# A two-block transformer on one core: background steps held back from a feed-forward layer's first granules, and the second mixer's norm outputs, bias rows and constants placed elsewhere

## The chip, the core and the metric

The kernel runs on one core of a Trainium2 chip. The core has a matmul engine (TensorE, PE in the profile; its weight loads are PEld), three elementwise engines (VectorE is DVE, ScalarE is ACT, GpSimd is POOL), a sync engine (SP) that issues most of the loads, and 16 DMA engines. Each engine takes its instructions strictly in the order of its own queue, so an instruction that waits holds up all that stand behind it. The metric is the device time of one execution in microseconds (us); lower is better.

## The reference

One sequence of 256 tokens of width 1024 passes two blocks, all in float32. The first block has two layers, each of four steps with a layer norm behind the first, second and last:

```python
x = layer_norm(ALPHA*x + 0.5*swiglu(x, ffn1_up, ffn1_down))   # width 2816
x = layer_norm(ALPHA*x + token_mix(x))                        # four branches, gates, w_out
x = x + ple_gate(x) * (p @ w_ple)
x = layer_norm(ALPHA*x + 0.5*swiglu(x, ffn2_up, ffn2_down))
```

The second block begins with a modulation that depends on one vector c alone:

```python
mod = silu(c) @ w_ada + b_ada                  # 6 x 1024: shift, scale, gate; twice
h = rms_norm(x, norm_mix) * (1 + sc_m) + sh_m
x = x + g_m * hybrid_mixer(h, ...)             # differential attention, LRU, sliding window
h = rms_norm(x, norm_ffn) * (1 + sc_f) + sh_f
x = x + g_f * moe_ffn(h, ...)                  # 32 experts
```

The hybrid mixer needs a table of relative-position biases (`rel_bias`, by distance), a scalar and a gain for the differential attention, and products of query and key gains.

## The kernel before, in words

The 256 tokens are two tiles t of 128. A float32 product is made of three matmuls: each weight and each activation is split into a high part (`hi`, on ACT, L161, tile `whi`) and the rest (`lo`, L165, tile `wlo`), and PE adds xh*hi, xh*lo and xl*hi (L223 to L225). Weights come in **granules** of 128 x 1024: SP loads one into `raw` (4 buffers), ACT and DVE split it into `whi` and `wlo` (7 buffers, and 4 more in an extra pool while a feed-forward layer runs). `onpool` names the granules of a product whose `lo` half is split on POOL instead of DVE.

A feed-forward layer (`ffn`) goes through its 2816 columns in six blocks; each block has a product with the first half of the up weights and one with the second half, 8 granules in all. On DVE the first is gated (L325) and multiplied with the second (L329), and PE transposes the result (L251, tile `th`). The first block makes both products for t=0 and then for t=1 (`gemms`); its granules on POOL are `pl1` for the first half and `pl2` for the second. Then come 22 granules of down weights; the last eight are used for all of t=0 and then for all of t=1, and the layer norm of a tile follows its last product: residual (L284), statistics (L285, L287), a reciprocal root of small steps (L142 to L156), scaling (L292, L293), transposes (L251).

The modulation is computed beside the first block: `ada` is a generator that multiplies 32 pieces of `w_ada` (tile `araw`, two buffers) by c and adds them up in `acc`, one piece a step (L842), eight steps to an `acc`. It runs as three background jobs (`self.bg`): in the first layer's first feed-forward (`ada(0, 4)`), its second (`ada(4, 8)`) and the second layer's first (`ada(8, 12)`). After each granule that it loads, `load_split` calls `self.background(1)`, which runs the job to its next `yield`.

This sets the order in which the program is written. A scheduler then orders each engine's queue by what is ready in its own reckoning; an instruction that is not tied by data can move ahead of what is written before it. `pin` keeps an instruction in the order in which it was written.

At the end of the first block `load_first` loads the first product of the mixer and `norm_first` computes its norm (L879, L884, L885) into two of the four `raw` buffers. `hybrid` then makes the bias rows (`rel_rows`: two small matmuls, L995, and DMAs through DRAM), the products dq and dk for t=0 and t=1, dv, the differential attention (`diff_attn`, with its constants; the key norm ends with L1067), then r, the LRU and the window attention. The mixture of experts follows; it streams its weights in tiles of 1 MB (`mraw`) into memory that the earlier stages free.

Of the kernel before, what the change touches and what calls it, by code (L numbers as in the profile page):

```python
# [71 lines left out]
class Kernel:  # L72
    def __init__(self, tc, a, out, dbg=None):
        self.tc, self.nc, self.a, self.out, self.dbg = tc, tc.nc, a, out, dbg
        self.n = 0
        self.nraw, self.nhl, self.next, self.xp = 4, 7, 4, None
        self.npj, self.ngt, self.glag = 4, 4, 1
        self.dtail = 8
        self.xg = 4
        self.sp, self.late = None, False  # L80
        self.pre, self.npre = [], 5
        self.start = False
        self.na, self.nb = 8, 9
# [726 lines left out]
    def ada(self, r0, r1):  # L810
# [3 lines left out]
        with self.tc.tile_pool(name=self.nm("ada"), bufs=1, side="right") as pool:  # L814
# [169 lines left out]
    def rel_rows(self, mp):  # L984

        nc, a = self.nc, self.a
        rel = self.st(mp, [33, 12], "rel")
        nc.vector.memset(rel[32:33, :], -1e30)
        nc.gpsimd.dma_start(rel[0:32, :], a["rel_bias_2"])
        oh = self.st(mp, [33, 2, 384], "s4")  # L990
        nc.gpsimd.dma_start(oh, a["bucket"])
        row = self.st(mp, [12, 2, 384], "s4")
        for i in range(2):
            pr = self.ps("sc")
            nc.tensor.matmul(pr[:12, :384], rel, oh[:, i, :], start=True, stop=True)  # L995
# [33 lines left out]
    def gain128(self, a1, a2):  # L1029
# [6 lines left out]
        gp = self.small(1, "g1")  # L1036
        self.pin(nc.vector.tensor_tensor(gp, g[:, 0:1], g[:, 1:2], op=OP.mult))
        return gp

    def diff_attn(self, mp, dq, dk, dv):  # L1040
        nc, a = self.nc, self.a
        lv = self.st(mp, [P, 4, 64], "s2")
        src = a["diff_lambda_2"][0]
        nc.gpsimd.dma_start(lv, bass.AP(tensor=src.tensor, offset=src.offset, ap=[[0, P], [64, 4], [1, 64]]))
        lp = self.st(mp, [P, 2, 64], "s2")
        nc.vector.tensor_tensor(lp, lv[:, 0::2, :], lv[:, 1::2, :], op=OP.mult)
        ls = self.small(2, "lz")
        nc.vector.tensor_reduce(ls, lp, axis=AX.X, op=OP.add)
        nc.scalar.activation(ls, ls, AF.Exp)
        nlam = self.small(1, "nl")  # L1050
        nc.vector.tensor_tensor(nlam, ls[:, 1:2], ls[:, 0:1], op=OP.subtract)
        nc.vector.tensor_scalar(nlam, nlam, -LAMBDA_INIT, None, op0=OP.add)
        gsub = self.st(mp, [P, P], "s2")
        nc.gpsimd.dma_start(gsub, arow(a["diff_subln_2"][0], P))
        nc.vector.tensor_scalar(gsub, gsub, 1.0 - LAMBDA_INIT, None, op0=OP.mult)
        gp = self.gain128(a["diff_qnorm_2"][0], a["diff_knorm_2"][0])
# [71 lines left out]
    def swa(self, mp, sq_, kv):  # L1128
# [3 lines left out]
        gp = self.gain128(a["swa_qnorm_2"][0], a["swa_knorm_2"][0])  # L1132
# [61 lines left out]
    def hybrid(self, ctx, first):  # L1194
# [3 lines left out]
        with tc.tile_pool(name="mix2", bufs=1, reuse_waits="tile") as mp:  # L1198
            self.mod_cols()

            self.st(mp, [33, 12], "rel")
# [8 lines left out]
            with tc.tile_pool(name="scr", bufs=1, reuse_waits="tile") as self.sp:  # L1210
                self.rel_rows(mp)
                dq, dk = self.projs(mp, lhs, w, (1024, 512, (), first), (1536, 512, (2, 3), None))
# [5 lines left out]
                for i in range(2):  # L1218
                    r = self.proj(mp, lhs, w, i * 512, 512, onpool=(1, 3))
# [613 lines left out]
    def run(self):  # L1833
        nc, a, tc = self.nc, self.a, self.tc
        with tc.tile_pool(name="const", bufs=1) as self.cp, tc.tile_pool(name="small", bufs=2) as self.smp, \
# [15 lines left out]
            def load_first():  # L1851
                first.extend(self.load_split(KD, a["w_in_2"][0], 1024, 512, onpool=(1,2,3)))

            def norm_first(t):
                if self.dbg != "ln3_1":
                    hs.append(self.st(self.wp, [P, D], "raw", bufs=self.nraw))
                    self.rms_mod(t, hs[t], A, sh)

            with tc.tile_pool(name="ln", bufs=1) as self.lnp:
                pl, self.pl1, self.pl2 = (self.pl1, self.pl2), (), ()  # L1860
                for L in range(2):
# [3 lines left out]
                    if L:  # L1865
                        self.bg = self.ada(8, 12)
# [11 lines left out]
                    if L == 0:  # L1878
                        self.bg = self.ada(4, 8)
# [56 lines left out]
```

## Time and profile before

| what | value |
|---|---|
| time, median of 3 runs (lowest to highest) | 2527.62 us (2524.69 to 2527.79) |
| the profiled execution: its own time, its span | 2525.59 us, 2524.0 us |
| granted TensorE clock, mean | 0.98 |
| busy: PE, DVE, ACT, POOL | 95%, 52%, 33%, 8% |
| moved by DMA | 705.94 MB, mean 280 GB/s |

The span begins with the first instruction of the execution and ends with the last; times within it are counted from its start. The layer norms that matter here end at about 217 and 225 us (layer 0, first feed-forward), 666 and 684 us (layer 0, second) and 1306 and 1320 us (layer 1, second); the mixture of experts runs from about 1556 us to the end.

### The profile page before, as it was taken

The numbers are of one execution on the slowest core, as the hardware profiler recorded it, in microseconds if no ns is written. First come the engines' busy times: TensorE is split into PE (matmuls) and PEld (weight loads), VectorE is DVE, ScalarE is ACT, GpSimd is POOL, SyncE is SP. The second block draws the span as 40 slices with busy tenths as digits, with TensorE's granted clock in tenths as the row PEclk, the third lists the DMA queues.
The fourth block names the chain that finished last, engine by engine and source line by source line (L and its number), as shares of the span: only waits on it lengthen the run. The fifth ranks groups of instructions, "written<-read, shape, count | busy, mean of one in ns | idle before, by whom it ended". The sixth has DMA issues, their size and how long they took to land.

```text
span 2524.0 us, 29376 instructions
## 1 busy us (share of the span) xinstructions
PE 2389.5 (95%) x11078; PEld 1562.4 (62%) x11078; DVE 1313.9 (52%) x2243; ACT 827.1 (33%) x1227; POOL 209.1 (8%) x191
## 2 busy tenths in 40 slices
PE   8998999999799999999988999999999999999998
PEld 6887787778678878878877877433333333333332
DVE  7768757666666676675566775322222222222222
ACT  5443544444345454444435753100000001000000
POOL 4000211200200011230013010000000000000000
PEclk9999999999899999999998999999999999999999
DMA  8777465567666656566547467999999999999997
GB/s 272 242 236 233 144 188 182 184 215 222 210 188 215 217 159 175 171 197 195 184 131 232 118 199 289 399 421 421 420 421 421 420 421 420 420 421 421 421 421 325
DMA packets 202027, 705.94 MB, mean 280 GB/s; under 512 B 18122, under 2 KB 31642, under 8 KB 152984
## 3 DMA queue, kind: packets, MB, share of 16 engines
q1 hardware_dynamic: 194584, 684.02, 74.1%
q0 software_dynamic: 7296, 19.99, 2.7%
q8 instruction: 89, 1.46, 0.2%
q14 instruction: 58, 0.48, 0.1%
HBM read 702.83 MB, written 3.47 MB: 280 GB/s over the span
## 4 chain that ended last, share of the span: by engine, by line
PE 53%; DMA 31%; DVE 9%; issue 3%; ACT 3%; POOL 1%; SPq 0%; ACTq 0%; DVEq 0%; POOLq 0%
DMA mraw<-in_w_dram 25%; PE mm L225 12%; PE mm L224 12%; PE mm L223 12%; PE mm L1590 5%; PE sc L1621 4%; PE tp L251 3%; DVE wlo L165 2%; DMA araw<-in_w_ada_dram 2%; DMA raw<-in_ffn_up_dram 2%; ACT whi L161 1%; DMA raw<-in_w_in_dram 1%; PE tp L1700 1%; PE sc L1519 1%; DVE x L292 1%
## 5 line engine op out<-in xcount | busy, mean ns | idle before, releaser
L165 DVE TENSOR_TENSOR wlo<-raw,whi 128x1024 fp32r<-128x1024 f32 (+1 forms) x451 | 559.0, 1246 | 277.2 <-ACT whi L161 274.5
L161 ACT ACTIVATE whi<-raw 128x1024 fp32r<-128x1024 f32 x478 | 500.7, 1055 | 521.5 <-PE mm L225 386.3
L224 PE MATMUL mm<-wlo,xTh 128*128 128x512 f32 (+2 forms) x1520 | 580.4, 382 | 10.6 <-POOL wlo L165 8.6
L223 PE MATMUL mm<-whi,xTh 128*128 128x512 f32 (+2 forms) x1520 | 585.8, 386 | 2.1 <-ACT whi L161 1.7
L225 PE MATMUL mm<-whi,xTl 128*128 128x512 f32 (+2 forms) x1520 | 579.8, 382 | 0.0
L1590 PE MATMUL mm<-mraw,xe 128*64 128x512 f32 x1920 | 488.5, 613 | 33.6 <-DMA mraw<-in_w_dram 33.5
L1590 PEld LDWEIGHTS mm<-mraw,xe 128*64 128x64 f32 x1920 | 150.6, 141 | 332.6 <-issue 265.2
L224 PEld LDWEIGHTS mm<-wlo,xTh 128*128 128x128 f32 x1520 | 288.6, 190 | 69.8 <-POOL wlo L165 11.5
L223 PEld LDWEIGHTS mm<-whi,xTh 128*128 128x128 f32 x1520 | 289.0, 190 | 56.2 <-ACT whi L161 3.0
L225 PEld LDWEIGHTS mm<-whi,xTl 128*128 128x128 f32 x1520 | 288.6, 190 | 50.0
L1601 ACT ACTIVATE mt<-mg 128x256 f32<-128x256 f32 x64 | 26.6, 416 | 691.5 <-DVE mg L1600 689.5
L1621 PE MATMUL sc<-mraw,xTl 128*64 128x512 f32 x976 | 231.5, 597 | 7.4 <-ACT xe L1530 7.4
L1600 DVE TENSOR_SCALAR mg<-mm 128x256 f32<-128x256 f32 x64 | 27.2, 424 | 323.4 <-PE mm L1590 319.0
L1621 PEld LDWEIGHTS sc<-mraw,xTl 128*64 128x64 f32 x976 | 69.1, 137 | 125.6 <-issue 108.9
L225 PE MATMUL mm<-whi,hl 128*128 128x512 f32 x352 | 138.1, 392 | 0.0
L223 PE MATMUL mm<-whi,hh 128*128 128x512 f32 x352 | 137.6, 391 | 0.0
L224 PE MATMUL mm<-wlo,hh 128*128 128x512 f32 x352 | 137.5, 391 | 0.0
L1626 DVE TENSOR_TENSOR xTh<-sc,gf 128x512 f32<-128x512 f32 x32 | 22.1, 692 | 208.4 <-PE sc L1621 208.4
L1701 DVE TENSOR_TENSOR x<-x,tp 128x512 f32<-128x512 f32 x68 | 46.8, 688 | 129.8 <-PE tp L1700 129.8
L842 DVE SCALAR_TENSOR_TENSOR acc<-araw,cond,acc 128x512 f32<-128x512 f32 x96 | 72.8, 758 | 54.2 <-DMA araw<-in_w_ada_dram 51.8
L165 POOL TENSOR_TENSOR wlo<-raw,whi 128x1024 fp32r<-128x1024 f32 x27 | 68.9, 2564 | 285.6 <-ACT whi L161 285.5
L225 PEld LDWEIGHTS mm<-whi,hl 128*128 128x128 f32 x352 | 66.4, 189 | 13.6
(445 smaller groups left out, 2277.5 us busy)
## 6 DMA issues: line engine op xcount, KB each, us to landing
mraw<-in_w_dram SPq DMA_DIRECT2D x360, 1024.0 KB, 19.8
raw<-in_ffn_up_dram SPq DMA_DIRECT2D x176, 512.0 KB, 4.4
raw<-in_w_in_dram SPq DMA_DIRECT2D x142, 512.0 KB, 4.4
raw<-in_ffn_down_dram SPq DMA_DIRECT2D x88, 512.0 KB, 4.0
araw<-in_w_ada_dram SPq DMA_DIRECT2D x96, 256.0 KB, 3.6
AS<-in_w_dram SPq DMA_DIRECT2D x22, 1024.0 KB
raw<-in_w_branch_dram SPq DMA_DIRECT2D x28, 512.0 KB, 3.9
raw<-in_w_out_dram SPq DMA_DIRECT2D x16, 512.0 KB, 3.7
```

What stands on the lines that cost most here:

```text
L161: ins = self.nc.scalar.activation(hi, src, AF.Copy)
L165: ins = (self.nc.gpsimd if pool else self.nc.vector).tensor_tensor(lo, src, hi, op=OP.subtract)
L223: nc.tensor.matmul(banks[b], xh, hi[:, s], start=kc == 0, stop=False)
L224: nc.tensor.matmul(banks[b], xh, lo[:, s], start=False, stop=False)
L225: nc.tensor.matmul(banks[b], xl, hi[:, s], start=False, stop=kc == nk - 1)
L251: self.nc.tensor.transpose(pt[:s.shape[-1], i * P:i * P + s.shape[0]], s, self.ident)
L842: nc.vector.scalar_tensor_tensor(acc, raw, self.cond[:, k:k + 1], acc, op0=OP.mult, op1=OP.add)
L1590: self.pe(nc.tensor.matmul(ph[nb][e * 64:e * 64 + 64], xe[:, k, e * 64:e * 64 + 64], units[e][k][:, nb * 512:nb * 512 + 512], start=False, ...
L1600: nc.vector.tensor_scalar(g, pv[:, :, 0], 7.0, None, op0=OP.min)
L1601: nc.scalar.activation(th, g, AF.Tanh, scale=0.851)
L1621: self.pe(self.nc.tensor.matmul(py[c][e * 64:e * 64 + 64], aT[:, k:k + 64], units[e][j][:, o:o + 512], start=j == 0 and r == 0, stop=j == ...
L1701: nc.vector.tensor_tensor(self.x[t][:, s], self.x[t][:, s], po, op=OP.add)
```

## The change

Eight edits, in the order of the file. `pl1` loses both granules on POOL and `pl2` two of four. `self.hold` lets the first 12 calls of `background(1)` pass without a step, for `ada(4, 8)` and `ada(8, 12)`. `ada` yields once before its first step and once a step (before: twice behind every second one), and its first step is pinned. After the last job come the bias rows and the constants of the differential attention, with `araw` and `acc` as their working tiles and lasting tiles (`self.cp`) for their results; some of their arithmetic goes to POOL. The products of gains are made there too. `load_first` has granule 3 on DVE, dk has no granule on POOL, the first r product has none. `norm_first` writes into `whi` buffers of the extra pool.

```diff
-        self.pl1, self.pl2 = (2, 3), (0, 1, 2, 3)
-        self.bg = iter(())
+        self.pl1, self.pl2 = (), (1, 3)
+        self.bg, self.hold = iter(()), 0
...
     def background(self, n):
+        if n == 1 and self.hold:
+            self.hold -= 1
+            return
         for _ in range(n):
...
             nxt, last, ahead = start(r0), None, load(r0 * KD)
+            yield
...
-                    nc.vector.scalar_tensor_tensor(acc, raw, self.cond[:, k:k + 1], acc, op0=OP.mult, op1=OP.add)
+                    ins = nc.vector.scalar_tensor_tensor(acc, raw, self.cond[:, k:k + 1], acc, op0=OP.mult, op1=OP.add)
+                    if (i, k) == (r0, 0):
+                        self.pin(ins)
...
                     yield
-                    if j % 2:
-                        yield
                 last = i, acc
             yield
             finish(*last)
+            if r1 == 12:
+                yield
+                yield from self.rel_rows(lambda: self.st(pool, [P, 512], "araw", bufs=2),
+                                         lambda: self.st(pool, [P, 512], "acc", bufs=2))
...
-    def rel_rows(self, mp):
+    def rel_rows(self, one, two):
...
         for i in range(2):
-            pr = self.ps("sc")
-            nc.tensor.matmul(pr[:12, :384], rel, oh[:, i, :], start=True, stop=True)
-            nc.scalar.activation(row[:, i, :], pr[:12, :384], AF.Copy)
-        dr = self.dram.tile([12, 768], F32, name="relrow")
-        nc.gpsimd.dma_start(dr, row.rearrange("p a b -> p (a b)"))
+            oh = one()[:33, :384]
+            nc.gpsimd.dma_start(oh, a["bucket"][:, i])
+            row = two()[:12, :384]
+            pr = self.ps("tp")
+            nc.tensor.matmul(pr[:12, :384], rel, oh, start=True, stop=True)
+            nc.scalar.activation(row, pr[:12, :384], AF.Copy)
+            nc.gpsimd.dma_start(dr[:, i * 384:i * 384 + 384], row)
+            yield
...
+        nc.gpsimd.tensor_tensor(lp, lv[:, 0::2, :], lv[:, 1::2, :], op=OP.mult)
+        yield
+        ls = self.small(2, "lz")
+        self.pin(nc.vector.tensor_reduce(ls, lp, axis=AX.X, op=OP.add))
...
-                dq, dk = self.projs(mp, lhs, w, (1024, 512, (), first), (1536, 512, (2, 3), None))
+                dq, dk = self.projs(mp, lhs, w, (1024, 512, (), first), (1536, 512, (), None))
...
-                    r = self.proj(mp, lhs, w, i * 512, 512, onpool=(1, 3))
+                    r = self.proj(mp, lhs, w, i * 512, 512, onpool=(1, 3) if i else ())
...
-                first.extend(self.load_split(KD, a["w_in_2"][0], 1024, 512, onpool=(1,2,3)))
+                first.extend(self.load_split(KD, a["w_in_2"][0], 1024, 512, onpool=(1, 2)))
...
-                    hs.append(self.st(self.wp, [P, D], "raw", bufs=self.nraw))
+                    hs.append(self.st(self.xp, [P, D], "whi", F32R, bufs=self.next).bitcast(F32))
...
-                        self.bg = self.ada(8, 12)
+                        self.bg, self.hold = self.ada(8, 12), 12
...
-                        self.bg = self.ada(4, 8)
+                        self.bg, self.hold = self.ada(4, 8), 12
```

The diff alone does not show what becomes of the queues, so three places of DVE's queue follow. **Place 1**, before: the layer norm of t=0 at the end of layer 0's second feed-forward (`x_71` is the activation of t=0, `mm` a product, `acc` and `araw` the background job's tiles).

```order
L284 SCALAR_TENSOR_TENSOR x_71<-mm_5353,x_71 128x512
L285 BN_STATS bn_1201_5573<-x_71 128x6
L842 SCALAR_TENSOR_TENSOR acc_5925<-araw_6014,cond,acc_5925 128x512
L842 SCALAR_TENSOR_TENSOR acc_5925<-araw_6029,cond,acc_5925 128x512
L284 SCALAR_TENSOR_TENSOR x_71<-mm_5354,x_71 128x512
L842 SCALAR_TENSOR_TENSOR acc_5925<-araw_6038,cond,acc_5925 128x512
```

The same place in the changed kernel:

```order
L284 SCALAR_TENSOR_TENSOR x_71<-mm_5353,x_71 128x512
L285 BN_STATS bn_1201_5573<-x_71 128x6
L284 SCALAR_TENSOR_TENSOR x_71<-mm_5354,x_71 128x512
L285 BN_STATS bn_1201_5573<-x_71 128x6
L287 BN_AGGR mv_1202_5578<-bn_1201_5573 128x2
```

No background step stands in this norm any more; the same holds at the end of layer 0's first feed-forward. **Place 2**, before: the third block of layer 0's second feed-forward, from the gating of one product (L325) to the multiplication (L329) that its transposes wait for. `wlo` is the split of a granule on DVE.

```order
L325 SCALAR_TENSOR_TENSOR th_4541<-th_4541,mm_4491 128x512
L842 SCALAR_TENSOR_TENSOR acc_4556<-araw_4580,cond,acc_4556 128x512
L325 SCALAR_TENSOR_TENSOR th_4544<-th_4544,mm_4492 128x512
L842 SCALAR_TENSOR_TENSOR acc_4556<-araw_4659,cond,acc_4556 128x512
L165 TENSOR_TENSOR wlo_4671<-raw_4668,whi_4670 128x1024
L165 TENSOR_TENSOR wlo_4680<-raw_4677,whi_4679 128x1024
L842 SCALAR_TENSOR_TENSOR acc_4556<-araw_4674,cond,acc_4556 128x512
L842 SCALAR_TENSOR_TENSOR acc_4556<-araw_4683,cond,acc_4556 128x512
L165 TENSOR_TENSOR wlo_4745<-raw_4742,whi_4744 128x1024
L842 SCALAR_TENSOR_TENSOR acc_4556<-araw_4754,cond,acc_4556 128x512
L329 TENSOR_TENSOR th_4541<-th_4541,mm_4583 128x512
```

In the changed kernel the fourth block reads as follows, and the fifth likewise (L328 and L332 are the old L325 and L329, L846 is the old L842):

```order
L328 SCALAR_TENSOR_TENSOR th_4724<-th_4724,mm_4674 128x512
L846 SCALAR_TENSOR_TENSOR acc_4662<-araw_4736,cond,acc_4662 128x512
L328 SCALAR_TENSOR_TENSOR th_4727<-th_4727,mm_4675 128x512
L846 SCALAR_TENSOR_TENSOR acc_4662<-araw_4745,cond,acc_4662 128x512
L165 TENSOR_TENSOR wlo_4856<-raw_4853,whi_4855 128x1024
L846 SCALAR_TENSOR_TENSOR acc_4662<-araw_4754,cond,acc_4662 128x512
L165 TENSOR_TENSOR wlo_4865<-raw_4862,whi_4864 128x1024
L846 SCALAR_TENSOR_TENSOR acc_4662<-araw_4763,cond,acc_4662 128x512
L165 TENSOR_TENSOR wlo_4877<-raw_4874,whi_4876 128x1024
L846 SCALAR_TENSOR_TENSOR acc_4662<-araw_4842,cond,acc_4662 128x512
L165 TENSOR_TENSOR wlo_4942<-raw_4939,whi_4941 128x1024
L332 TENSOR_TENSOR th_4724<-th_4724,mm_4766 128x512
```

Before, half of each of the two later jobs stands ahead of its layer, in the norm before it and the work around that, and the other 16 steps are spread over the third to the fifth block; now all 32 steps stand between the first block and the first down granules. The second block has ten steps in a row between the L332 of the first block and its own, five of them behind its L328. **Place 3**, before: the end of the first block, where the norm of t=0 for the mixer (L884, L885) stands ahead of the residual of t=1 (`x_72`).

```order
L156 SCALAR_TENSOR_TENSOR ry_2378_10985<-rt_2380_10989,ry_2378_10985 128x1
L884 SCALAR_TENSOR_TENSOR raw_10974<-x_71,ry_2378_10985,AS_9538 128x512 x2
L885 TENSOR_TENSOR raw_10974<-raw_10974,AS_9538 128x512 x2
L284 SCALAR_TENSOR_TENSOR x_72<-mm_10728,x_72 128x512
L285 BN_STATS bn_2385_11064<-x_72 128x6
```

In the changed kernel the residual and statistics of t=1 stand among the root of that norm (L887 is the old L879), and three granules of dk stand in the layer norm of t=0 ahead of them:

```order
L165 TENSOR_TENSOR wlo_11234<-raw_11231,whi_11233 128x1024
L156 SCALAR_TENSOR_TENSOR ry_2380_11006<-rt_2382_11010,ry_2380_11006 128x1
L152 SCALAR_TENSOR_TENSOR rt_2382_11010<-ry_2380_11006,rh_2381_11008 128x1
L156 SCALAR_TENSOR_TENSOR ry_2380_11006<-rt_2382_11010,ry_2380_11006 128x1
L293 SCALAR_TENSOR_TENSOR x_71<-x_71,ry_2380_11006,lnb_10616 128x512 x2
L284 SCALAR_TENSOR_TENSOR x_72<-mm_10777,x_72 128x512
L887 TENSOR_TENSOR sr_2386_11024<-sr_2386_11024 128x1
L284 SCALAR_TENSOR_TENSOR x_72<-mm_10778,x_72 128x512
L142 TENSOR_SCALAR rv_2389_11030<-sr_2386_11024 128x1
L285 BN_STATS bn_2398_11113<-x_72 128x6
```

What was one norm behind the other is now the two in turns, with L892 and L893 (the old L884 and L885) of t=0 behind both L292 of t=1.

## Rows read from the trace of the kernel before

**Rows 1.** Windows: length, busy PE, PEld, DVE, ACT, POOL, granted clock, DMA share, GB/s.

```profile
190.00:240.00 50.00, 42.79 (x193) 36.32 (x192) 38.53 (x79) 18.90 (x29) 2.69 (x5) 0.90 0.68 218
640.00:700.00 60.00, 45.54 (x193) 37.28 (x192) 41.76 (x62) 20.97 (x25) 15.84 (x8) 0.89 0.60 189
850.00:890.00 40.00, 39.74 (x190) 33.68 (x189) 26.42 (x52) 16.82 (x24) 2.71 (x5) 1.00 0.52 165
1296.00:1384.00 88.00, 72.64 (x316) 58.05 (x314) 62.81 (x125) 38.19 (x68) 26.21 (x22) 0.90 0.53 171
1556.00:2524.00 968.00, 911.09 (x4080) 350.78 (x4078) 259.70 (x632) 87.44 (x227) 0.52 (x1) 0.97 1.00 413
```

**Rows 2.** Waits of PE, 190 to 240 us: us in total, times, longest.

```profile
PE tp L251 <- DVE x L293: 7.2, 1, 7.2
```

**Rows 3.** Waits of PE, 640 to 700 us.

```profile
PE tp L251 <- DVE x L293: 14.5, 2, 8.1
```

**Rows 4.** Timeline of DVE, 634 to 712 us: start, us, [idle before].

```profile
653.79 2.60 DVE L842 SCALAR_TENSOR_TENSOR acc<-araw,cond,acc 128x512 f32<-128x512 f32 x2 [7.09 <-DMA araw<-in_w_ada_dram]
...
660.57 0.74 DVE L292 SCALAR_TENSOR_TENSOR x<-x,mv,lng 128x512 f32<-128x512 f32 x1
...
673.92 2.32 DVE L292 SCALAR_TENSOR_TENSOR x<-x,mv,lng 128x512 f32<-128x512 f32 x1
```

**Rows 5.** Timeline of POOL, 640 to 700 us.

```profile
670.92 7.56 POOL L165 TENSOR_TENSOR wlo<-raw,whi 128x1024 fp32r<-128x1024 f32 x3 [15.87 <-ACT whi L161]
```

**Rows 6.** Waits of PE, whole span.

```profile
PE mm L224 <- POOL wlo L165: 8.6, 7, 1.6
...
PE tp L251 <- DVE raw L885: 6.1, 2, 3.4
...
PE tp L251 <- DVE s L1067: 5.5, 1, 5.5
...
PE sc L995 <- ACT sc L878: 1.5, 1, 1.5
```

**Rows 7.** Timeline of PE, 1296 to 1330 us.

```profile
1310.69 1.94 PE L251 MATMUL tp<-ident,raw 128*128 128x128 f32 x8 [2.74 <-DVE raw L885]
...
1325.37 1.94 PE L251 MATMUL tp<-ident,raw 128*128 128x128 f32 x8 [3.38 <-DVE raw L885]
```

**Rows 8.** Window of DVE, 1297.3 to 1325.4 us: length, busy.

```profile
1297.30:1325.40 28.10, 25.35 (x75) 0.92 0.19 50
```

**Rows 9.** Timeline of DVE, 1350 to 1364 us.

```profile
1355.66 2.38 DVE L154 TENSOR_TENSOR rt<-ry 128x32 f32<-128x32 f32 x1
...
1358.53 0.19 DVE L154 TENSOR_TENSOR rt<-ry 128x32 f32<-128x32 f32 x1
```

**Rows 10.** Waits of PE, 440 to 640 us.

```profile
PE mm L224 <- POOL wlo L165: 3.9, 3, 1.6
PE tp L251 <- DVE th L329: 3.0, 1, 3.0
```

**Rows 11.** Waits of PE, 700 to 860 us.

```profile
PE tp L251 <- DVE th L329: 1.3, 1, 1.3
```

**Rows 12.** Groups by form: xcount | busy, mean ns of one | idle before.

```profile
L842 DVE SCALAR_TENSOR_TENSOR acc<-araw,cond,acc 128x512 f32<-128x512 f32 x96 | 72.8, 758 | 54.2 <-DMA araw<-in_w_ada_dram 51.8 <-DMA acc<-in_b_ada_dram 1.8 <-DVE wlo L165 0.2
...
L165 DVE TENSOR_TENSOR wlo<-raw,whi 128x1024 fp32r<-128x1024 f32 x443 | 551.0, 1251 | 272.6 <-ACT whi L161 270.0
...
L165 POOL TENSOR_TENSOR wlo<-raw,whi 128x1024 fp32r<-128x1024 f32 x27 | 68.9, 2564 | 285.6 <-ACT whi L161 285.5
```

**Rows 13.** Timeline of DVE, 490 to 560 us: background steps.

```profile
526.87 0.75 DVE L842 SCALAR_TENSOR_TENSOR acc<-araw,cond,acc 128x512 f32<-128x512 f32 x1
...
546.98 0.75 DVE L842 SCALAR_TENSOR_TENSOR acc<-araw,cond,acc 128x512 f32<-128x512 f32 x1
```

**Rows 14.** Timeline of PE, 459.8 to 480 us.

```profile
459.83 0.39 PE L225 MATMUL mm<-whi,xTl 128*128 128x512 f32 x1
...
471.61 0.39 PE L223 MATMUL mm<-whi,xTh 128*128 128x512 f32 x1
```

More of the change, by code (lines that the diff above doesn't have):

```diff
@@ L982, in lru @@
             self.split_from(h[:, :, t * P:t * P + P], yT[t][0], yT[t][1])
-    def rel_rows(self, mp):
+    def rel_rows(self, one, two):
         nc, a = self.nc, self.a
-        rel = self.st(mp, [33, 12], "rel")
-        nc.vector.memset(rel[32:33, :], -1e30)
+        rel = self.cp.tile([33, 12], F32, name="rel")
+        nc.gpsimd.memset(rel[32:33, :], -1e30)
         nc.gpsimd.dma_start(rel[0:32, :], a["rel_bias_2"])
-        oh = self.st(mp, [33, 2, 384], "s4")
-        nc.gpsimd.dma_start(oh, a["bucket"])
-        row = self.st(mp, [12, 2, 384], "s4")
+        dr = self.dram.tile([12, 768], F32, name="relrow")
         for i in range(2):
-            pr = self.ps("sc")
-            nc.tensor.matmul(pr[:12, :384], rel, oh[:, i, :], start=True, stop=True)
-            nc.scalar.activation(row[:, i, :], pr[:12, :384], AF.Copy)
-        dr = self.dram.tile([12, 768], F32, name="relrow")
-        nc.gpsimd.dma_start(dr, row.rearrange("p a b -> p (a b)"))
+            oh = one()[:33, :384]
[6 more added lines that the diff above has]
+            yield
         self.skew = []
@@ L1005, in rel_rows @@
             self.skew.append(sk)
+        yield
+        lv, lp = one(), two()
+        lv, lp = lv[:, :256].rearrange("p (i d) -> p i d", i=4), lp[:, :128].rearrange("p (i d) -> p i d", i=2)
+        src = a["diff_lambda_2"][0]
+        nc.gpsimd.dma_start(lv, bass.AP(tensor=src.tensor, offset=src.offset, ap=[[0, P], [64, 4], [1, 64]]))
+        nc.gpsimd.tensor_tensor(lp, lv[:, 0::2, :], lv[:, 1::2, :], op=OP.mult)
+        yield
+        ls = self.small(2, "lz")
+        self.pin(nc.vector.tensor_reduce(ls, lp, axis=AX.X, op=OP.add))
+        nc.scalar.activation(ls, ls, AF.Exp)
+        yield
+        self.nlam = self.cp.tile([P, 1], F32, name="nlam")
+        self.pin(nc.vector.tensor_tensor(self.nlam, ls[:, 1:2], ls[:, 0:1], op=OP.subtract))
+        nc.vector.tensor_scalar(self.nlam, self.nlam, -LAMBDA_INIT, None, op0=OP.add)
+        self.gsub = self.cp.tile([P, P], F32, name="gsub")
+        nc.gpsimd.dma_start(self.gsub, arow(a["diff_subln_2"][0], P))
+        nc.gpsimd.tensor_scalar(self.gsub, self.gsub, 1.0 - LAMBDA_INIT, None, op0=OP.mult)
+        self.gp = [self.gain128(a[f"{n}_qnorm_2"][0], a[f"{n}_knorm_2"][0]) for n in ("diff", "swa")]
     def rel_tile(self, dst, h0, nh, swa):
@@ L1035, in gain128 @@
                 nc.gpsimd.dma_start(g[b:b + 64, i:i + 1], src.rearrange("(p o) -> p o", o=1))
-        gp = self.small(1, "g1")
-        self.pin(nc.vector.tensor_tensor(gp, g[:, 0:1], g[:, 1:2], op=OP.mult))
+        gp = self.cp.tile([P, 1], F32, name=self.nm("gp"))
+        nc.gpsimd.tensor_tensor(gp, g[:, 0:1], g[:, 1:2], op=OP.mult)
         return gp
@@ L1041, in diff_attn @@
         nc, a = self.nc, self.a
[L1042 to L1056, printed above, removed]
+        nlam, gsub, gp = self.nlam, self.gsub, self.gp[0]
         bias = self.st(mp, [P, 4, 256], "s4")
@@ L1131, in swa @@
         nc.gpsimd.dma_start(sink, arow(a["swa_sinks_2"][0], 8))
-        gp = self.gain128(a["swa_qnorm_2"][0], a["swa_knorm_2"][0])
+        gp = self.gp[1]
         bias = [self.st(mp, [P, 4, 256], "s4") for _ in range(2)]
```

2 lines of the change are left out of this document (removed).

## The prediction, before the run

> **What bounds the kernel now.** The table of times says PE 95% busy, but that is an average, so I read the windows by stage first [rows 1]. The last 968 us are another kernel: the DMA engines are at a share of 1.00 there, at 413 GB/s, and no edit touches that stream. It starts in memory that the stages ahead of it free, so what they gain or lose, the end gains or loses. Ahead of it PE is the bound wherever nothing is late: the norm from 850 to 890 us leaves PE idle 0.3 us of 40. The same kind of place from 190 to 240 us leaves 7.2, that from 640 to 700 leaves 14.5, and the one into the second block (1296 to 1384) 15.4. So the change is judged by what ends PE's waits there, and the waits name it: the layer norm's last step, 7.2 us [rows 2] and 14.5 us [rows 3]; splits on POOL, the norm outputs, a small matmul and the key norm [rows 6]; and the multiplication L329 in the middle of two layers, 3.0 and 1.3 us [rows 10, 11].
>
> The reason for the two norms shows in DVE's queue. A background step stands between the halves of the residual (place 1), and DVE idles 7.09 us before it, for the `araw` transfer, while the product that it should add is long there [rows 4]. Later in the same norm L292 takes 2.32 us where its twin took 0.74 [rows 4]: POOL is splitting, 7.56 us for three granules [rows 5].
>
> Prices: a background step 0.758 us, a split 1.251 us on DVE and 2.564 on POOL [rows 12]; a matmul of 512 columns 0.2265 us (52 intervals between 459.83 and 471.61) [rows 14], so a product of both tiles, 48 matmuls, 10.9 us.
>
> **The change part by part**, against the profiled execution's own 2525.6 us (span 2524.0 and 1.6 around it; 2.0 below the median of the three runs).
>
> *A. Layer 0's first norm.* No background step stands in it now. The 7.2 us of [rows 2] should fall to the 0.3 of the norm at 850 us [rows 1]. The clock averages 0.90 over these 50 us, the idle stretch included, so about 1 us of slow matmuls goes too (estimate). **-8 us**; between -7 and -9.
>
> *B. Layer 0's last norm.* The first of two waits, 8.1 us, has the cause of A and goes. The second, 6.4, had three POOL splits under it; two of the six of this layer's first block stay on POOL, and by the queue both fall beside the norm of t=1. A split under it cost L292 2.32 - 0.74 = 1.6 us [rows 4]; I leave 2.5 us of wait for two with their rest, and take back 2 of slow clock (0.89 over 60 us). **-14 us**; from -9 (the second wait stays) to -16.
>
> The lock on a shared port is a rule of the Trainium skill (SBUF — State Buffer, section SBUF: two separate sides): a VectorE operation with two SBUF inputs and a GpSimd operation exclude each other for the whole instruction. By it the 17 splits taken from POOL would free up to 17 x 2.564 = 44 us of DVE; by the rows only those under a norm count, here some 5 us. I use the rows.
>
> *C. First block of the two second feed-forwards.* PE waits 3.9 us for POOL's splits in layer 0 [rows 10]; of the 8.6 in all [rows 6], 4.7 remain for layer 1 and the mixer. Six granules in a row at 2.564 us came too slowly for a pass over t=0 that uses one every six matmuls, 1.36 us. Now four of the six go to DVE at 1.251 us, under that pace; these 5 us of DVE hide beside PE, else they would be the new wait. I leave 0.8 us. **-7 us**; 0 to -7.8.
>
> *D. Into the second block.* Here the order gives with one hand. Both norms are one queue on DVE: 25.4 of 28.1 us busy between the residual of t=0 and the transposes of t=1 at 1325.37 [rows 7, 8]. Interleaving them (place 3) does not shorten the queue; three more splits (3.8 us) replace what POOL's stretching and the constants cost there, so the transposes of t=1 stay where they are, near 1325.4. Those of t=0, which need L893 now behind both L292 of t=1, come later: after 1308.0 (1310.69 - 2.74) I add the rows of the new queue, residuals and statistics 2.7, both roots 3.5, two L292, 1.4, L892 and half of L893, 2.0, some 9.5 us. So that gap grows from 2.7 to about 9.5 us, but the bias matmuls with their wait of 1.5 [rows 6] and the 3.4 ahead of t=1 fall into it, and PE reaches 1325.4 with the same products done. Gains come behind: dk's splits are ready (0.8 of the POOL waits), PE starts after t=1 without its second slow phase (about 2.5 us of the 0.90 over 88 us [rows 1], estimate), and the key norm, whose steps were stretched from 0.19 to 2.38 us [rows 9], has POOL only at its end, so of 5.5 us [rows 6] I leave 2. **-7 us**; from +3 (only the larger gap) to -10.
>
> *E. The background jobs.* Nothing is removed: 96 steps before and after. But 32 of them (16 of each later job) come from norms and mixers back into layers where PE is the bound, in runs. A step needs its `araw`, and two buffers give one step per 2.87 us (8 steps from 526.87 to 546.98) [rows 13]. Place 2 now has five steps between gating and L332: four intervals, a step and a split make 11.5 + 0.8 + 1.3 = 13.5 us, where PE needs 10.9 for the product; the transposes stand two or three matmuls behind it, so PE waits 2.6 less 0.6. The two such places before cost 3.0 and 1.3 [rows 10, 11], mean 2.15. In each later job two blocks have that form; the second block has ten steps in 21.8 us, 9 x 2.87 + 2.1 = 27.9, up to 6 late: I take 4. Twice 8.3, and once 2.15 in the first feed-forward, where steps come one per granule instead of two in three: 18.8, less the 4.3 of before. **+14 us**. From below: 0, if split granules ahead and earlier loads cover all, since the other groups of eight steps in these two layers made PE wait nowhere: L329 has one wait in each [rows 10, 11]. From above: every run pays its full rate, 16 steps at 2.87 against 11 granules at 2.72 (12 matmuls), 16 us, four times, with no cover: +60 after the 4.3.
>
> *F. Bias rows and constants* in layer 1's down granules: 2 small matmuls, two ACT copies, three small DVE operations behind POOL's DMAs. The splits ahead are the cover: PE takes 2.72 us a granule and DVE 1.25. Two of DVE's operations are pinned and can wait for POOL, whose queue has the two large bias copies ahead; behind them stand splits with several granules in hand. 0; without that cover some 3 us.
>
> Sum: -8 - 14 - 7 - 7 + 14 = -22, so **2503 us**.
>
> **The rivals.** *1. The background runs cost little (chance 0.15).* For it: most groups of eight steps cost nothing before [rows 10, 11]. E near 2: 2491 us. *2. They cost double (0.15),* because `araw` comes slower where a granule and a step share each 2.72 us (768 KB, 289 GB/s): E = 28, 2517 us. *3. The norms give back half (0.12):* POOL's two splits fall fully under the norm of t=1 and the gap at 1308 is not made up: B -9, D +3, 2518 us. *4. The runs become the bound (0.08):* from E above about 36 the gains are gone; at three quarters of its upper end, 46, the time is 2535 us, slower. It needs DVE late by 10 us at each of four runs, and then every `wlo` behind a step is late as well: seven split buffers hold some 19 us of PE's work, which speaks against it. *5. The change moves waits without shortening them (0.06):* each of PE's waits passes to DVE's other work, 2525 us.
>
> A page speaks against moving splits: the Trainium skill (Perfetto Trace Analysis, section Optimizing Scalar/DVE Operations) says that with VectorE saturated, work may go to ScalarE or even GpSimd, though it doubts that pair for the port. As a mechanism here that is C turned round: DVE, with 5 us more in a first block, lets `wlo` come late; if all 3.9 us stay in both layers, the time is 2510, inside the range. DVE is busy 38.5 of 50 us and 41.8 of 60 in the windows of the two norms [rows 1], not saturated, so this case has 0.04, within the forecast's share.
>
> **How the numbers follow.** The forecast (0.44) spans 2495 to 2512, its terms each a little off. With rivals 1 to 3, each some 4 us to either side, the range becomes **2487 to 2521**; rivals 4 and 5 (0.14) and the far sides of the others (0.06) stay out. A change of 0.2%, 5 us, is about what a measurement of this kernel can tell from none. Faster by more (below 2522): the forecast and rivals 1 to 3, 0.86. Same: rival 5, 0.06. Slower: rival 4, 0.08.
>
> **What will show it.** A: no wait on L293 near 215 us. B: one wait under 4 us near 680. C: no wait on POOL splits near 475 and 1130. D: a gap near 9 us before the t=0 transposes of the mixer's norm, a small one before those of t=1, under 3 before the key's. E: PE waits for L332 at the second, fourth and fifth blocks of two layers, 12 to 20 us together. It is wrong if those waits reach 35, or if L293 still waits while no `araw` stands ahead of it.

## The result and the profile after

The changed kernel takes 2492.59 us (median of 4 runs, 2487.62 to 2498.68), the kernel before 2527.51 beside it: a ratio of 0.9865, 95% interval 0.985 to 0.9881, or 35 us. Its profiled execution is the slowest of the four, 2498.68 us with a span of 2497.0, 27 us less than that of before.

The waits of PE in the whole span (us in total, times, longest):

```profile
PE tp L251 <- DVE th L332: 14.4, 10, 4.0
PE tp L251 <- DVE whi L893: 7.4, 2, 7.2
PE tp L251 <- DVE x L293: 6.4, 5, 2.1
...
PE tp L251 <- DVE s L1117: 2.3, 1, 2.3
...
PE tp L251 <- DVE s L1080: 2.0, 1, 2.0
```

No wait on POOL's splits is left of the 8.6 us in [rows 6]. L332, the multiplication inside the feed-forwards, now leads: the price that was paid. The windows that answer to [rows 1], with the columns given there:

```profile
183.00:232.00 49.00, 48.75 (x230) 41.09 (x230) 33.72 (x62) 22.41 (x32) 2.69 (x5) 1.00 0.63 191
640.00:690.00 50.00, 47.78 (x221) 38.91 (x220) 37.48 (x63) 21.38 (x25) 5.88 (x4) 1.00 0.54 176
690.00:720.00 30.00, 25.96 (x107) 21.18 (x106) 21.61 (x27) 10.78 (x13) 0.00 (x0) 0.89 0.80 255
1278.00:1366.00 88.00, 76.31 (x343) 61.53 (x342) 65.35 (x132) 41.88 (x76) 8.15 (x8) 0.92 0.46 143
```

Layer 0's two feed-forward norms (first two rows) leave PE idle 0.3 and 2.2 us, at the full granted clock of 2.4 GHz, where [rows 1] had 7.2 and 14.5 us and a mean of 0.90 and 0.89, that is with stretches at 1.2 GHz. In the third row PE waits inside layer 1's first feed-forward and the clock falls with it. PE's timeline names the single waits:

```profile
429.83 0.59 PE L251 MATMUL tp<-ident,x 128*128 128x128 f32 x2 [2.13 <-DVE x L293]
...
508.39 1.11 PE L251 MATMUL tp<-ident,th 128*128 128x128 f32 x4 [2.53 <-DVE th L332]
...
666.76 0.63 PE L251 MATMUL tp<-ident,x 128*128 128x128 f32 x4 [2.08 <-DVE x L293]
...
707.38 1.11 PE L251 MATMUL tp<-ident,th 128*128 128x128 f32 x4 [4.04 <-DVE th L332]
...
1297.08 1.94 PE L251 MATMUL tp<-ident,whi 128*128 128x128 f32 x8 [7.15 <-DVE whi L893]
...
1305.06 0.63 PE L251 MATMUL tp<-ident,whi 128*128 128x128 f32 x4 [0.22 <-DVE whi L893]
...
1336.48 0.63 PE L251 MATMUL tp<-ident,s 128*128 128x128 f32 x4 [1.98 <-DVE s L1080]
```

**Time by stage.** PE's transposes of `th` stand in every kernel in the same order (28 places), and so do the last ones of `pj` ahead of the mixture of experts (1544.55 us before, 1518.30 after). The differences of their start times, kernel less kernel before, give what each stage gained or lost in the profiled executions. The edges are 147.4, 492.8, 599.9, 704.7, 810.1, 1247.7 and 1544.6 us of before.

| stage (what it holds) | forecast | changed | again | background alone | splits alone | rest alone | four araw |
|---|---|---|---|---|---|---|---|
| first feed-forward (E) | +2.2 | +3.3 | +2.3 | +2.2 | +1.4 | +0.1 | +1.2 |
| to layer 0's second (A, C) | -11.5 | -12.3 | -14.9 | -9.8 | -2.9 | -2.1 | -14.1 |
| layer 0's second (E) | +5.3 | +1.8 | +3.7 | +3.8 | -0.8 | -1.4 | -2.2 |
| its last norm (B) | -14 | -16.2 | -14.6 | -8.8 | -3.5 | +0.2 | -15.1 |
| layer 1's first (E) | +7.0 | +8.1 | +5.4 | +5.9 | -0.5 | +0.5 | -0.3 |
| rest of layer 1 (C, F) | -3.5 | -3.0 | -2.8 | +1.1 | -4.8 | +1.5 | -3.1 |
| second mixer (D) | -7 | -8.0 | -6.9 | +2.8 | -1.0 | -8.1 | -10.7 |
| to the end | 0 | -0.8 | +0.4 | 0.0 | 0.0 | -0.7 | -0.9 |

"Rest alone" has no edit in its first two stages and still shows +0.1 and -2.1: a stage is known to about 2 us.

### The profile page after: what moved, and what is told of

It reads as the page before. It is cut to its first block, busy times and chain, and to the rows that moved or that the text cites. A ratio compares the mean times of both kernels' runs of the same rounds, so it can differ in the third digit from the quotient of the medians.

```text
span 2497.0 us, 29400 instructions
## 1 busy us (share of the span) xinstructions
PE 2383.5 (95%) x11078; PEld 1559.5 (62%) x11078; DVE 1308.9 (52%) x2255; ACT 828.7 (33%) x1227; POOL 169.9 (7%) x181
## 4 chain that ended last, share of the span: by engine, by line
PE 48%; DMA 34%; DVE 10%; issue 4%; ACT 3%; POOL 1%; DVEq 0%; SPq 0%; ACTq 0%; POOLq 0%
DMA mraw<-in_w_dram 28%; PE mm L225 12%; PE mm L224 12%; PE mm L223 12%; PE mm L1601 4%; DVE wlo L165 3%; DMA araw<-in_w_ada_dram 3%; PE sc L1632 3%; PE tp L251 2%; DMA raw<-in_ffn_up_dram 1%; ACT whi L161 1%; PE tp L1711 1%; DVE acc L846 1%; DMA raw<-in_w_ple_gate_dram 0%; DMA acc<-in_b_ada_dram 0%
## 5 line engine op out<-in xcount | busy, mean ns | idle before, releaser
L165 DVE TENSOR_TENSOR wlo<-raw,whi 128x1024 fp32r<-128x1024 f32 (+1 forms) x468 | 580.6, 1248 | 262.9 <-ACT whi L161 260.9
L846 DVE SCALAR_TENSOR_TENSOR acc<-araw,cond,acc 128x512 f32<-128x512 f32 x96 | 71.8, 748 | 46.8 <-DMA araw<-in_w_ada_dram 40.5
L223 PEld LDWEIGHTS mm<-whi,hh 128*128 128x128 f32 x352 | 66.1, 188 | 13.8 <-issue 0.6
```

What stands on the lines that cost most here:

```text
L165: ins = (self.nc.gpsimd if pool else self.nc.vector).tensor_tensor(lo, src, hi, op=OP.subtract)
L223: nc.tensor.matmul(banks[b], xh, hi[:, s], start=kc == 0, stop=False)
L846: ins = nc.vector.scalar_tensor_tensor(acc, raw, self.cond[:, k:k + 1], acc, op0=OP.mult, op1=OP.add)
```

## The experiments

They ran in three groups of four, the first two groups on one chip and the third on another, each group beside the kernel before (2526.38, 2527.60 and 2529.01 us); ratios are compared across them.

**1. The background edit alone.** The kernel before with the edit below, and the hold for `ada(4, 8)` likewise:

```diff
+        if n == 1 and self.hold:
+            self.hold -= 1
+            return
...
+            yield
...
+                    if (i, k) == (r0, 0):
+                        self.pin(ins)
...
-                    if j % 2:
-                        yield
...
-                        self.bg = self.ada(8, 12)
+                        self.bg, self.hold = self.ada(8, 12), 12
```

> The kernel before with the background edit alone (the hold of 12 calls, one yield ahead of the first step, one a step, the pin). If the steps' places make the gain of the two norms and the price in the layers, as the two traces read: first norm -10, first wait of layer 0's last norm with its slow matmuls -10, and +13 for the waits on L332 in the three layers, so 2520 us, and the second wait near 680 us, under POOL's splits, stays at about 6 us. If the splits on POOL made the gain of the norms, only the price is left: 2540 us, with a wait above 6 us at both norms.

2520.66 us, ratio 0.9965 (0.9951 to 0.998). PE at layer 0's last norm, for t=0 and t=1:

```profile
654.03 0.63 PE L251 MATMUL tp<-ident,x 128*128 128x128 f32 x4 [2.38 <-DVE x L293]
...
671.24 1.09 PE L251 MATMUL tp<-ident,x 128*128 128x128 f32 x4 [4.79 <-DVE x L293]
```

The first wait falls from 8.1 us [rows 3] to 2.38; the one under POOL's splits stays long, 4.79 us. The time is as expected: of the 18.6 us that the stages of the two norms gain, the three stages marked E take back 11.9.

**2. The splits alone.** The kernel before with the four changed lists of granules on POOL:

```diff
-        self.pl1, self.pl2 = (2, 3), (0, 1, 2, 3)
+        self.pl1, self.pl2 = (), (1, 3)
...
-                dq, dk = self.projs(mp, lhs, w, (1024, 512, (), first), (1536, 512, (2, 3), None))
+                dq, dk = self.projs(mp, lhs, w, (1024, 512, (), first), (1536, 512, (), None))
```

and those of the first r product and of `load_first`.

> The kernel before with the changed places of splits alone (pl1, pl2, dk, the first r product, the mixer's first product). By my account: no wait on POOL's splits at the two first blocks, -8, the second wait of layer 0's last norm shorter by 3 to 6, and 1 to 3 behind the second block's norm: 2511 to 2514 us, with the first norm's wait of 7.2 us and the first of 8.1 near 666 us still there. If the splits were the cause of the long norms: both waits fall too, and the time is 2495 us or less.

2513.36 us, ratio 0.9942 (0.9925 to 0.9958). The first norm, and the two waits of layer 0's last:

```profile
216.80 1.94 PE L251 MATMUL tp<-ident,x 128*128 128x128 f32 x8 [6.12 <-DVE x L293]
...
664.55 1.08 PE L251 MATMUL tp<-ident,x 128*128 128x128 f32 x4 [8.17 <-DVE x L293]
...
682.65 0.63 PE L251 MATMUL tp<-ident,x 128*128 128x128 f32 x4 [2.48 <-DVE x L293]
```

The complement of experiment 1: the waits behind background steps stay, the one under POOL's splits falls from 6.4 to 2.48. The two causes at this norm are shown apart.

**3. No hold.** The changed kernel with

```diff
-                        self.bg, self.hold = self.ada(8, 12), 12
+                        self.bg, self.hold = self.ada(8, 12), 0
```

and the same for `ada(4, 8)`.

> The changed kernel with both holds at 0, so that the two later jobs may step from the first granule on. By my account steps return to the two norms and leave the layers: +20 at the norms, -9 in the layers, 2503 us, with a wait on L293 of 6 us or more at one norm at least. If the pin on the first step alone keeps the norms free, or if the runs in the layers cost more than the norms give: 2480 to 2490 us.

2496.44 us, ratio 0.9874 (0.9858 to 0.9891), which can't be told from the changed kernel: I was 7 us too high. At layer 0's last norm the waits return (3.37 and 4.69 us, the stage gains 7.1 instead of 16.2), and PE waits 2.40 us at 465.89 us for a split on DVE, in the stage marked A, C, which gains 9.1 instead of 12.3. The three stages marked E cost 4.1 us instead of 13.2, and the second mixer gains 12.0 instead of 8.0, which I can't explain. The first norm stays free without the hold, as no step stands in it:

```profile
454.30 0.75 DVE L846 SCALAR_TENSOR_TENSOR acc<-araw,cond,acc 128x512 f32<-128x512 f32 x1
```

This is the second job's first step, the 33rd in the trace. In the kernel before it started at 201.20 us (shown in experiment 5), and half of the job ran from there to the 250s of us, through the norm at 217. So at the first norm the cure is in the other half of the edit, the pin on the first step or the changed yields; these two weren't tried apart.

**4. Four araw buffers.** The changed kernel with

```diff
-                raw = self.st(pool, [P, 512], "araw", bufs=2)
+                raw = self.st(pool, [P, 512], "araw", bufs=4)
```

in `ada` and where `rel_rows` is called.

> The changed kernel with four araw buffers in place of two. If two buffers set the pace of the runs of steps (a step per 2.5 to 2.9 us), PE's waits on L332, 14.4 us, fall to 4 or less, and the time by 10 to 14 us with their slow matmuls: 2480 us. If DVE's own work or the transfers' bandwidth sets it, the waits stay above 10 us: 2490 to 2495 us.

2479.73 us, ratio 0.9811 (0.9793 to 0.9828): faster than the changed kernel and clear of its interval. The groups of the steps in the changed kernel, then in this one (times and busy us, mean ns, idle before):

```profile
L846 DVE SCALAR_TENSOR_TENSOR acc<-araw,cond,acc 128x512 f32<-128x512 f32 x96 | 71.8, 748 | 46.8 <-DMA araw<-in_w_ada_dram 40.5 <-DMA acc<-in_b_ada_dram 5.2 <-DVE wlo L165 1.0
```

```profile
L846 DVE SCALAR_TENSOR_TENSOR acc<-araw,cond,acc 128x512 f32<-128x512 f32 x96 | 71.6, 747 | 9.3 <-DMA araw<-in_w_ada_dram 7.7 <-DMA acc<-in_b_ada_dram 0.6
```

and PE's waits on L332 in this one:

```profile
PE tp L251 <- DVE th L332: 3.5, 6, 1.1
```

DVE's idle time ahead of the steps falls from 46.8 to 9.3 us, PE's waits on L332 from 14.4 to 3.5, and the three stages marked E from +13.2 to -1.3 in sum. So two buffers, not DVE's work, made the price of the runs. The queue's order moved a little with the buffers: in layer 1's second block four steps stand between the gating and L332, where the changed kernel has five. What the order alone gives wasn't tried.

**5. Four araw buffers in the kernel before.** The same edit on the kernel before.

> The kernel before with four araw buffers in place of two, and nothing else. If the steps in the two norms cost by their wait for araw (DVE idle 7.09 us ahead of one), most of what the hold gave at the norms comes from this alone: the waits of 7.2 and 8.1 us on L293 fall to 3 or less, those on L329 to 1, and the time to 2508 to 2513 us. If the steps cost by their place in the queue, whatever they wait for: 2522 us or more.

2517.20 us, ratio 0.9965 (0.9951 to 0.9978): the gain is smaller than I expected. The first norm's wait is gone, the waits at layer 0's last norm stay at 7.43 and 4.85 us. DVE there, and then SP's queue, which issues the loads:

```profile
636.94 0.69 DVE L285 BATCH_NORM_STATS2 bn<-x 128x6 f32<-128x512 f32 x1
644.64 4.82 DVE L842 SCALAR_TENSOR_TENSOR acc<-araw,cond,acc 128x512 f32<-128x512 f32 x4 [7.01 <-DMA araw<-in_w_ada_dram]
649.38 0.69 DVE L284 SCALAR_TENSOR_TENSOR x<-mm,x 128x512 f32<-128x512 f32 x1
```

```profile
627.09 13.56 SPq L237 DMA_DIRECT2D raw<-in_ffn_up_dram  x7
640.70 9.12 SPq L833 DMA_DIRECT2D araw<-in_w_ada_dram  x8
```

DVE idles 7.01 us for `araw`, as it did with two buffers (7.09) [rows 4]: the job's loads stand behind seven granule loads of the next layer, which wait their turn for `raw`, from 627 to 640 us. More buffers didn't help a load that was issued late; a later step did. The first norm began the same way. In the kernel before, two steps stood ahead of its residual, and their loads were issued behind seven granule loads as well; SP's queue, then DVE:

```profile
182.11 11.76 SPq L237 DMA_DIRECT2D raw<-in_w_in_dram  x7
193.98 0.26 SPq L828 DMA_DIRECT2D acc<-in_b_ada_dram  x1
194.28 1.03 SPq L833 DMA_DIRECT2D araw<-in_w_ada_dram  x2
...
201.20 1.54 DVE L842 SCALAR_TENSOR_TENSOR acc<-araw,cond,acc 128x512 f32<-128x512 f32 x2 [6.39 <-DMA araw<-in_w_ada_dram]
```

With four buffers this norm is free, but no step stands in it any more: the second job's first step comes at 408.60 us. The scheduler's order changed there, so this run doesn't show what four buffers would do for a step that stays in the first norm.

**6. The changed kernel again,** with no edit.

> The changed kernel as it is, beside the others on one chip. Its profiled execution was the slowest of its four runs (2498.68, median 2492.6). If the runs of steps that wait for araw make the spread, a faster profile has waits on L332 well under the 14.4 us, and the other stages as they were. If the last stage makes it, the landmarks up to 1518 us agree within 2 us and the rest differs. Median 2490 to 2495 us.

2494.21 us, ratio 0.9867 (0.9845 to 0.9889). The profiled execution is again near the upper end, 2498.31 us of 2488.24 to 2499.39; its stages stand in the table. What the shorter executions have less is in no trace.

**7. Four buffers and no hold.** Experiments 3 and 4 together:

```diff
-                        self.bg, self.hold = self.ada(8, 12), 12
+                        self.bg, self.hold = self.ada(8, 12), 0
...
-                raw = self.st(pool, [P, 512], "araw", bufs=2)
+                raw = self.st(pool, [P, 512], "araw", bufs=4)
```

> The changed kernel with four araw buffers and both holds at 0. If the hold is worth its place once the steps no longer wait for araw, this loses some of the norms' gain (steps of 0.75 us and their splits stand in them again) and finds nothing left to win in the layers: 2484 to 2490 us. If four buffers do what the hold does: 2478 to 2482 us.

2487.53 us, ratio 0.9845 (0.9829 to 0.9861), slower than experiment 4 by 8.6 us by the ratios. With two buffers the hold was worth nothing that can be told; with four it keeps its gain, because the layers no longer take it back: the stages of the two norms gain 18.8 us here and 29.1 in experiment 4, and those marked E sum to -1.2 and -1.3.

**8. The norm of t=0 first.** The changed kernel with this in `layer_norm`:

```diff
+            if last and t:
+                self.pin(ins)
```

where `ins` is the residual (L284) of t=1.

> The changed kernel with the residual of t=1 pinned behind the whole norm of t=0 in the last norm of the first block, as it stood before. If the interleaving only moves PE's wait (7.15 us ahead of t=0's transposes now), that wait falls to 2 or 3 us, 3 to 5 us of wait appear ahead of t=1's transposes, and the time stays within 2 us of the changed kernel's. If the interleaving earns the gain of this stage: 5 us or more slower. If it costs: 3 us or more faster.

2493.39 us, ratio 0.9868 (0.9851 to 0.9884): no difference. PE's two waits, where the changed kernel has 7.15 and 0.22:

```profile
1290.19 1.94 PE L251 MATMUL tp<-ident,whi 128*128 128x128 f32 x8 [4.48 <-DVE whi L895]
...
1305.99 1.80 PE L251 MATMUL tp<-ident,whi 128*128 128x128 f32 x8 [2.37 <-DVE whi L895]
```

6.85 us against 7.37: the order passes part of the wait from one tile to the other, less of it than I expected (4.48 us stay ahead of t=0, where I had 2 to 3).

**9. The norm's outputs in `raw` again.** The changed kernel with

```diff
-                    hs.append(self.st(self.xp, [P, D], "whi", F32R, bufs=self.next).bitcast(F32))
+                    hs.append(self.st(self.wp, [P, D], "raw", bufs=self.nraw))
```

> The changed kernel with the outputs of the mixer's norm back in two of the four raw buffers. If that placing is what lets dk's granules be loaded and split ahead, a wait for dk's first granules appears behind the norm (2 to 3 us), the stage from 1248 us to the end of the mixer loses 4 to 6 us, and the time is 2497 us. If it only names another memory: 2492 to 2494 us.

2494.40 us, ratio 0.9860 (0.9846 to 0.9874): no difference; the waits are 1.38 and 6.36 us, and the norm of t=0 stands first here too, as in experiment 8. By itself this part of the change earns nothing that can be told.

**10. The rest alone.** The changed kernel with the diffs of experiments 1 and 2 taken back: bias rows, constants and norm outputs are left.

```diff
-        self.pl1, self.pl2 = (), (1, 3)
+        self.pl1, self.pl2 = (2, 3), (0, 1, 2, 3)
...
-                        self.bg, self.hold = self.ada(4, 8), 12
+                        self.bg = self.ada(4, 8)
```

> The kernel before with what the first two experiments left out: the norm outputs in the extra pool's buffers, the bias rows and constants made in layer 1, the products of gains, all splits and background steps as before. If the three parts add up, this must be worth what the other two (6 and 13 to 14 us) leave of 34: 2513 us. By the stages of the traces it is 4 to 8 us: 2520 to 2523 us, and the remainder belongs to a norm in which two parts are needed together (layer 0's last).

2521.24 us, ratio 0.9970 (0.9959 to 0.9981), as the second account had it. The mixer's first 88 us and the key norm's wait:

```profile
1296.00:1384.00 88.00, 74.40 (x345) 59.55 (x344) 68.57 (x129) 43.23 (x78) 22.62 (x15) 0.96 0.47 147
```

```profile
1356.25 0.63 PE L251 MATMUL tp<-ident,s 128*128 128x128 f32 x4 [1.65 <-DVE s L1079]
```

PE is idle 13.6 us instead of 15.4 and the mean granted clock is 0.96 instead of 0.90 [rows 1], some 5 us of 88 (estimate), so most of the stage's 8.1 us is clock. The key norm waits 1.65 us instead of 5.5 [rows 6] with dk's splits still on POOL; in experiment 2, with dk's on DVE and the constants in their old place, it waits 3.91. With experiments 8 and 9, by which order and memory of the norms change nothing, that points to the bias rows, constants and products of gains as what earned this stage; they weren't tried without the rest. By the ratios the three parts alone are worth 0.35, 0.58 and 0.30%, 1.23 together, of 1.35 for the whole.

**11. dk's splits behind the norm,** with four buffers: dk's DVE splits pinned in written order.

```diff
+            if self.behind:
+                self.pin(ins)
```

in `split_from`; `behind` is set around the products dq and dk.

> The changed kernel with four araw buffers, and dk's splits on DVE pinned in the order in which they are written, behind the mixer's norm of both tiles. If the three dk splits (3.8 us) in that norm cost PE time, the wait ahead of t=0's transposes falls from 7.1 us to 1 or less, the other grows little, and the time is 2475 to 2477 us. If they only pass the wait on to dk's first product: 2479 to 2481 us.

2483.26 us, ratio 0.9817 (0.9805 to 0.983): no gain over experiment 4. The waits are 1.45 and 6.31 us; the order of the two norms came back as in experiment 8 too, so the splits alone weren't tried.

**12. None of the first block's splits on POOL,** with four buffers:

```diff
-        self.pl1, self.pl2 = (), (1, 3)
+        self.pl1, self.pl2 = (), ()
```

> The changed kernel with four araw buffers and none of the first block's splits on POOL. If POOL's two splits under layer 0's last norm still cost (one DVE split there takes 3.21 us instead of 1.22), the 2.1 us of wait near 659 us falls under 1 and the time to 2476 to 2478 us. If DVE, with two more splits in each first block, comes late there, PE waits for its splits: 2482 to 2486 us.

2486.94 us, ratio 0.9833 (0.9821 to 0.9846), 5.6 us above experiment 4 by the ratios, though the intervals still touch. The wait at layer 0's last norm doesn't fall, it grows to 6.71 us; DVE ahead of it:

```profile
659.56 0.15 DVE L156 SCALAR_TENSOR_TENSOR ry<-rt,ry 128x1 f32<-128x1 f32 x1
663.10 1.23 DVE L165 TENSOR_TENSOR wlo<-raw,whi 128x1024 fp32r<-128x1024 f32 x1 [3.39 <-ACT whi L161]
664.24 1.41 DVE L293 SCALAR_TENSOR_TENSOR x<-x,ry,lnb 128x512 f32<-128x512 f32 x2
```

The root was done at 659.7, but a split whose `whi` wasn't there yet stood ahead of the norm's last step. No first block came late (no wait on its splits), so it was neither of my two accounts: a split on DVE cost here by what it waited for in the queue, as a background step did.

## Why the prediction was right, and where its steps were off

The range held and the sign was right; the forecast, 2503 us, is 10 us too high. Rival 1's number, 2491, is nearer, but its cause is not: it had the runs of steps at 2 us, and they cost 11.4 and 13.2 in the two profiles of the changed kernel. Both profiled executions, 2498.68 and 2498.31 us, are only 4 to 5 us below the forecast: the stages of A and C and of B gave 1 to 3 us more than forecast, and E cost 1 to 3 less. The rest is the distance from these executions to the medians, which no trace explains.

**A** was mis-sized by its clock. The wait went as forecast, 7.2 to under 0.3 us, but I took 1 us for the slow clock. The kernel before, in the wait and behind it:

```profile
211.60:216.60 5.00, 0.00 (x0) 0.00 (x0) 5.00 (x13) 0.00 (x0) 0.00 (x0) 0.50 0.95 333
216.60:221.80 5.20, 5.16 (x17) 4.66 (x18) 4.99 (x12) 2.14 (x3) 0.00 (x0) 0.50 0.50 178
```

A mean of 0.90 over 50 us [rows 1] is 10 us at 1.2 GHz. PE idled in half of them, where the clock costs nothing, and worked 5.2 us in the rest, so the price is 2.6 us (estimate) and the term some -9.5. The background edit alone, whose stage has A without C, shows -9.8.

**B** was right in size (-14.6 and -16.2) and in its two causes; the one wait left is 2.08 us against the 2.5 forecast. One DVE split under POOL's takes 3.21 us there where others take 1.22:

```profile
654.37 4.76 POOL L165 TENSOR_TENSOR wlo<-raw,whi 128x1024 fp32r<-128x1024 f32 x2 [53.25 <-ACT whi L161]
...
657.01 3.21 DVE L165 TENSOR_TENSOR wlo<-raw,whi 128x1024 fp32r<-128x1024 f32 x1
...
664.54 1.22 DVE L165 TENSOR_TENSOR wlo<-raw,whi 128x1024 fp32r<-128x1024 f32 x1
```

By the lock that the Trainium skill describes (SBUF — State Buffer, section SBUF: two separate sides) the two engines exclude each other for a whole instruction. These rows agree: the split on DVE ends 1.1 us after POOL's second. The gain needs both edits: alone they give 8.8 and 3.5, together 14.6 to 16.2.

**C** was right within the 2 us of a stage: -7.7 for the splits alone over its two stages, -7 forecast, and no wait on POOL's splits is left.

**D** came out at its size (-7 forecast, -8.0 and -6.9), but by luck: the steps that I put under it don't carry it. The interleaved norms, the memory of the norm outputs and dk's splits on DVE change nothing that can be measured (experiments 2, 8 and 9). The gap ahead of t=0 is 7.15 us, not 9.5, and t=1's transposes come 2.0 us earlier relative to the last `th` transposes, not at the same place. What earned it, by experiment 10, is **F** seen from the other side: I counted what the bias rows and constants cost in their new place (0, which holds within the 2 us of a stage) and only 1.5 us of what they cost in the old one; there it is some 8. By the rows this is 1.8 us less idle time and less time at 1.2 GHz; which of F's operations mattered most wasn't tried.

**E** was right in size, 11.4 and 13.2 against 14, and experiment 4 shows the cause that the sum used: two buffers' rate. It was not split rightly, and part of the match is luck. The waits are shorter, 14.4 us in all where the sum had 18.8. But behind the two longest, 2.53 and 4.04 us, the clock falls to 1.2 GHz, which I hadn't counted. The waits in the kernel before, then the two stretches in the changed one:

```profile
PE tp L251 <- DVE th L329: 5.6, 4, 3.0
```

```profile
508.40:511.80 3.40, 3.40 (x12) 2.99 (x13) 3.13 (x5) 1.19 (x2) 0.00 (x0) 0.50 0.99 361
707.40:713.20 5.80, 5.80 (x18) 4.84 (x19) 4.91 (x7) 1.20 (x2) 0.00 (x0) 0.50 0.90 303
```

Half of these 9.2 us is 4.6 (estimate); with the 8.8 us more of waits that makes 13.4, where the stages have 13.2.

**What stays open.** The stages of both profiled executions of the changed kernel sum to -27 us, while the medians differ by 35. 2 us of it is the profiled execution of before, which was faster than its median; for the other 6 a shorter execution of the changed kernel would have to be profiled. The changed kernel's executions spread over 11 us. The waits for `araw` aren't shown as the source: experiment 9, with two buffers, spreads over 2.4 us, and experiments 4, 7 and 11, with four, over 6.2, 8.7 and 1.4.

The version that beats both kernels is experiment 4, 2479.73 us.

## What to carry to other kernels

When a wait on a norm is found, look in its engine's queue for the instruction that stands ahead and is itself waiting for a load, and then in the load's queue for why it is late. The two reasons here needed different cures: where the load was issued late (layer 0's last norm), more buffers changed nothing and a later step did; where two buffers set the pace of a run of steps (the layers), two more buffers took the price away. A buffer count can also change the order that a scheduler makes, so read the queue again before crediting the buffers. Work moved out of a critical stretch takes its own rate with it; before moving it, see whether its buffers let it run at the pace of its new place. And price a wait with the slow clock behind it: the first norm's 7.2 us cost some 10.

## What the runs showed of the hardware that was not expected

Waits of PE of nearly the same length had different consequences for the granted clock. After the 2.13 us at 429.83 the window from 425 to 440 us has a mean of 0.89, after the 2.08 us at 666.76 the windows from 664 to 668 and from 668 to 672 have 1.00:

```profile
425.00:440.00 15.00, 12.87 (x54) 10.44 (x54) 12.70 (x29) 7.27 (x10) 0.55 (x1) 0.89 0.50 151
...
664.00:668.00 4.00, 1.92 (x14) 1.41 (x13) 3.89 (x8) 2.69 (x3) 1.00 (x2) 1.00 0.81 281
668.00:672.00 4.00, 4.00 (x21) 3.30 (x20) 3.59 (x6) 2.92 (x5) 0.12 (x1) 1.00 0.86 307
```

So the price of a 2 us wait is 2 or 4 us (estimate: the wait, and where the clock fell 0.11 of 15 us). The place doesn't decide it. In the repeated kernel the first of these waits is 1.67 us and the clock stays at 1.00, the second is 2.11 us and it falls:

```profile
425.00:440.00 15.00, 13.30 (x66) 10.50 (x65) 13.74 (x33) 7.53 (x12) 1.08 (x2) 1.00 0.51 179
...
660.00:675.00 15.00, 12.89 (x56) 10.40 (x55) 12.85 (x24) 8.29 (x10) 1.12 (x2) 0.89 0.89 292
```

The stages go the same way: the repeated kernel is 2.6 us better in the stage of the first wait and 1.6 us worse in that of the second, differences about as large as the 2 us to which a stage is known.
